# Wider products for the filter taps, later loads of the attention constants, and new instruction orders in a two-layer encoder

## The chip, the core and the metric

The kernel runs on one core of a Trainium2 chip. A core has five engines that run side by side: TensorE (PE: matrix products; its weight loads are listed as PEld), VectorE (DVE), ScalarE (ACT), GpSimd (POOL) and SyncE (SP, which here only issues transfers). Each engine takes its instructions in order and waits at the head of its queue on semaphores. Transfers from device memory run on 16 DMA engines. The metric is the device time of one launch in microseconds (us), the median of several runs.

## The reference

A hybrid encoder of two layers on an input of 256 tokens by 1024 features, all in float32:

```python
for i in range(2):
    x = x + 0.5 * swiglu(rmsnorm(x, norm_g[i, 0]), ffn_w_gate[i, 0], ffn_w_up[i, 0], ffn_w_down[i, 0])
    h = rmsnorm(x, norm_g[i, 1])
    if i == 0:   # mixer: pooling over 4 windows | order-2 Hyena (long convolutions with generated filters)
        proj = h @ mix_w_in
        x = x + concat(pool_mixer(proj[:512]), hyena_mixer(proj[512:], spectra)) @ mix_w_out
    else:        # latent attention, 16 heads, low-rank q and kv, one rotary key
        x = x + mla_mixer(h, ...)
    x = x + 0.5 * swiglu(rmsnorm(x, norm_g[i, 2]), ffn_w_gate[i, 1], ffn_w_up[i, 1], ffn_w_down[i, 1])
return rmsnorm(x, final_norm_g)
```

A feed-forward block is `(silu(h @ w_gate) * (h @ w_up)) @ w_down` with 2816 hidden features. The Hyena filters come from a small network on position features: three layers of width 64 with a sine, then `h @ w_out` (64 to 2048: two orders, two directions, 512 channels), times a decay window, then normalised by energy and transformed. The product with `w_out` is what the code calls the taps.

## The kernel before

Every float32 product is made of three products in a reduced-precision float32 format: an operand is split into a high part and a low part, and high by high, low by high and high by low are summed (`mm3`, lines 265 to 267). A split is a copy on ScalarE (`split_hi`, line 246, tiles `wh`, `ph`, `xTh`) and a subtraction on VectorE or GpSimd (`split_lo`, line 250, tiles `wl`, `pl`, `xTl`). All weights are streamed from device memory in units of 1 MB: a transfer into one of two `raw` buffers, then the split into one of four `wh`/`wl` buffer pairs, then the products. There are four PSUM banks `mm` and four `acc`.

The stages follow one another on TensorE: first feed-forward block, mixer, second block, third block, attention, fourth block. The filter work of the mixer depends on no token, so its 21 steps (`filter_steps`) are hung into the first block: `FILTERS` gives for each step the number of the hook at which it is issued; one hook follows each gate/up chunk and each half of a down chunk. Hooks 5, 8 and 11 follow the gate/up products of chunks 2, 3 and 4; hooks 6 and 7 follow the two halves of down chunk 1, hooks 9 and 10 those of down chunk 2, hooks 12 and 13 those of down chunk 3. Steps 7 and 8 are `wout` (split of the last hidden layer and of `w_out`) and `taps(0)`; then come `energy(0)`, `taps(1)`, `energy(1)`, `norm(0)`, `scaled(0)`, `norm(1)`, the tables, `dft(0, 0)`, `dft(0, 1)`, `scaled(1)`, `dft(1, 0)`, `dft(1, 1)`.

In the taps, `lo` holds the low part of the hidden layer in partitions 64 to 127 and its full value in 0 to 63, so that `lo` by `wh` over 128 partitions gives two of the three products; the third is `hi` by `wl` over partitions 0 to 63.

In the mixer, in attention and at the very start every engine's order is written out by hand in a string (`START`, `MIX`, `MLA`); a token is a letter for an operation and numbers for its unit, piece or tile, and each engine takes its own instructions in the order of the string. In `MIX`: `I` loads a unit, `h` is a high piece on ScalarE, `l` and `g` are a low piece on VectorE and on GpSimd, `P` projects, `A` is the output product, `F` adds it to x, `J` transposes x for the next block and multiplies by its gain, `j` splits that, `B` and `R` make the norm's factor. Units 12 and 13 hold the first gate weights of the second block. In `MLA`: `C` compresses to the latents, `l` and `m` turn and split the last quarter of x, `a`, `b`, `c`, `d` are norm moments, rotary key, normalisation and split of the latents, `w`, `x` and `y` are high pieces and low pieces on VectorE and on GpSimd, `I` and `i` are the low parts of queries on GpSimd and VectorE, and `Y` and `z` those of the heads' outputs. `BUFFERS` lists which buffer each tile takes, in order of allocation.

In the feed-forward blocks the instructions are placed by the scheduler of the framework, which follows its own estimate of when operands are ready; the last quarter of x, `late_now`, is transposed there with high priority. That scheduler also places what stands outside the strings, such as the four transfers of attention's constants (`ckr`, `cqt` and the two halves of `gb`, lines 1002 to 1007, issued by GpSimd) and the clearing of the value tiles (line 1020, GpSimd): in the code they stand near the end of the third block, in the trace they run as soon as the memory of the mixer's tiles is free.

Of the kernel before, what the change touches and what calls it, by code (L numbers as in the profile page):

```python
# [12 lines left out]
F32 = mybir.dt.float32  # L13
# [8 lines left out]
P = 128  # L22
D = 1024
S = 256
# [20 lines left out]
)  # L45
MIX = (
# [11 lines left out]
)  # L58
MLA = (
# [16 lines left out]
)  # L76

FILTERS = 0, 3, 3, 3, 5, 5, 5, 6, 6, 7, 7, 7, 8, 9, 9, 10, 10, 10, 12, 13, 15

BUFFERS = {  # L80
    "mm": (
        "0123012301231023013132103213021302132013201320132012301230123012031203102310231023102312032103201320",
        "1302130213201320312031023102130231023102130213023102312031201320130213201320132120312012312132013021",
        "320313103210231203100132013201321032103201320123012310231032102",
    ),
    "acc": (
        "01230123012301320103123023102310231023102310231230310321032",
    ),
    "raw": (
        "0101010101010101010101010101010101010101010101010101010101010101010101010101010101010101010101010101",  # L90
        "010101010101010101010101010101010101010101010101010101010",
    ),
    "wh": (
        "0123012301230123012301230123012301230123021302130213021302130213021302130213021302130213021302130213",
        "0213021302130213021301230123012301230123012301230123012",
    ),
    "wl": (
        "0123012301230123012301230123012301230123021302130213021302130213021302130213021302130213021302130213",
        "0213021302130213021301230123012301230123012301230123012",
    ),  # L100
    "ph": (
        "012340123401234012342432014032410324103241032413024130241304213041240134203120342103421034210",
    ),
    "pl": (
        "012340123401234012342432014032410324103241032413024130241304213401204312041304120341203412034",
    ),
    "s": (
        "0120120120120120120120201201210212120102102101220120120120120120120120120120120120120120120121021021",
        "2010210210210210210212",
    ),  # L110
    "h": (
        "0123012301230123012301230123012301230123012301230123012302103210312310231023102",
    ),
    "cu": (
        "0110010110010101",
    ),
    "cv": (
        "011001010100",
    ),
    "cw": (  # L120
        "01010101011011001010",
    ),
}
MAGIC = 12582912.0
# [50 lines left out]
def turns(t):  # L175

    return slice(t, S, 2)


class Net:  # L180
# [391 lines left out]
    def filter_steps(self, hy, fl):  # L572

        nc, a = self.nc, self.a
# [64 lines left out]
        def wout():  # L639

            hi, lo = self.pl()
            nc.scalar.activation(hi[:, :S], st["h"], AF.Copy)
            nc.vector.tensor_tensor(out=lo[64:, :S], in0=st["h"][64:], in1=hi[64:, :S].bitcast(F32), op=ALU.subtract)
            nc.scalar.activation(lo[:64, :S], st["h"][:64], AF.Copy)
            st["h3"] = (hi, lo)
            st["wo"] = self.unit([(lambda raw, r=r: raw[r], a["hyena_ffn_w_out"][0]) for r in (slice(64), slice(64, P))], U)

        def taps(o):
            def go():
                hi, lo = st["h3"]  # L650
                wh, wl = st["wo"]
                for t in range(NT):
                    for d in range(2):
                        c = slice((2 * o + d) * W, (2 * o + d + 1) * W)
                        ps = self.bank()
                        nc.tensor.matmul(out=ps, lhsT=lo[:, turns(t)], rhs=wh[:, c], start=True, stop=False)
                        nc.tensor.matmul(out=ps, lhsT=hi[:64, turns(t)], rhs=wl[:64, c], start=False, stop=True)
                        e = E[o].rearrange("p (t x) s -> p t (x s)", t=2)[:, t, d * W:(d + 1) * W]
                        nc.vector.tensor_tensor(out=e, in0=ps, in1=e, op=ALU.mult)
            return go  # L660
# [330 lines left out]
            pre += units[12], units[13]  # L991


    def mla(self, ml, cur, nxt, wg, pre, hold, dump=None):

        nc, a, x = self.nc, self.a, self.x
        r, ms = cur["r"], cur["ms"]
# [1 line left out]
        NQ, NKV = 256, 160  # L999
        small = lambda name, n=2: ml.tile([P, n], F32, name=name, bufs=4)  # L1000
        ckr = ml.tile([P, 2, 64], F32, name="ckr")
        nc.gpsimd.dma_start(out=ckr, in_=a["c_kr"])
        cqt = ml.tile([P, 2, S], F32, name="cqt")
        nc.gpsimd.dma_start(out=cqt, in_=a["c_q"])
        gb = ml.tile([P, NQ + P], F32, name="gb")
        nc.gpsimd.dma_start(out=gb[:, :NQ], in_=a["mla_q_norm_g"].to_broadcast([P, NQ]))
        nc.gpsimd.dma_start(out=gb[:, NQ:], in_=a["mla_kv_norm_g"].to_broadcast([P, P]))

# [333 lines left out]
def encoder(ctx, tc, a, out, upto=99, dbg=None):  # L1342
    nc = tc.nc
# [101 lines left out]
    with tc.tile_pool(name="ml", bufs=1) as ml:  # L1445
        finish, mid = then(1, 1)
        _, nxt = then(1, 2)
        pre = [], []
        mla = N.mla(ml, mid, nxt, a["ffn_w_gate"][1, 1], *pre, None if upto > 5 else dump)
        ffn(1, 0, cur, finish if upto > 4 else dump, mid=lambda: next(mla))  # L1450
        if upto == 4:
            return
        for _ in mla:
            pass
        if upto == 5:
            return
        cur = nxt
# [28 lines left out]
```

## Time and profile before

| | |
|---|---|
| median of 3 runs | 978.87 us (977.22 to 979.04) |
| the profiled execution | 981.94 us; 980.1 us from its first to its last instruction |
| mean granted TensorE clock | 0.992 of full speed |
| PE busy | 959.8 us, 98% of the span |
| DVE, ACT, POOL busy | 595.3, 495.3, 181.3 us |

A busy PE is a union of overlapping matmuls, so it is not yet a full PE: how densely the starts of the products follow one another says more than the busy share.

### The profile page before, as it was taken

How to read it: one execution, taken by the hardware profiler on the slowest of the kernel's cores; microseconds unless marked ns; L12 is line 12 of the kernel's file. 1: busy time of each engine (PE TensorE's matmuls, PEld its weight loads, DVE VectorE, ACT ScalarE, POOL GpSimd, SP SyncE). 2: the span in 40 equal slices, each digit the busy share in tenths (PEclk: the TensorE clock that was granted, in tenths of full speed). 3: DMA queues.
4: the chain of work that ended last, by engine and by line, in shares of the span. 5: the costliest groups of instructions: out<-in, count | busy, mean ns of one | idle time of the engine just before them, and what ended most of it. 6: DMA issues, size and time to landing. Idle time of an engine off the chain costs nothing.

```text
span 980.1 us, 12375 instructions
## 1 busy us (share of the span) xinstructions
PE 959.8 (98%) x4792; PEld 804.6 (82%) x4792; DVE 595.3 (61%) x778; ACT 495.3 (51%) x780; POOL 181.3 (18%) x231
## 2 busy tenths in 40 slices
PE   9999999999999999999999999999899999999997
PEld 6878787889997788888888888888799988888885
DVE  5577677767886644554476445554677565454454
ACT  5565554446554544443454344444578665434442
POOL 1400433316665200000000000000256520000000
PEclk9999999999999899999999999999999999999999
DMA  7757566435234654565527654565142276556531
GB/s 258 239 177 217 181 206 210 157 102 158 82 127 142 224 206 171 172 215 204 182 90 253 207 180 172 172 214 182 55 135 86 88 236 215 179 178 213 203 129 43
DMA packets 80778, 168.09 MB, mean 172 GB/s; under 512 B 3820, under 2 KB 24181, under 8 KB 80336
## 3 DMA queue, kind: packets, MB, share of 16 engines
q1 hardware_dynamic: 79232, 164.79, 49.7%
q0 software_dynamic: 1200, 1.99, 0.8%
q8 instruction: 37, 0.61, 0.2%
q10 hardware_dynamic: 288, 0.52, 0.1%
q14 instruction: 21, 0.17, 0.0%
HBM read 165.72 MB, written 1.05 MB: 170 GB/s over the span
## 4 chain that ended last, share of the span: by engine, by line
PE 81%; DVE 8%; ACT 4%; DMA 3%; issue 3%; POOL 1%; SPq 0%; POOLq 0%; DVEq 0%; ACTq 0%
PE mm L265 16%; PE mm L266 16%; PE mm L267 16%; PE acc L267 8%; PE acc L266 8%; PE acc L265 8%; PE mm L270 4%; DVE wl L250 2%; DMA raw<-ffn_w_up 2%; ACT wh L246 2%; DMA raw<-mix_w_in 1%; DVE pl L250 1%; ACT ph L246 1%; DVE s L869 0%; PE mm L1267 0%
## 5 line engine op out<-in xcount | busy, mean ns | idle before, releaser
L250 DVE TENSOR_TENSOR wl<-raw,wh 128x1024 fp32r<-128x1024 f32 (+3 forms) x321 | 358.3, 1145 | 267.5 <-ACT wh L246 267.4
L246 ACT ACTIVATE wh<-raw 128x1024 fp32r<-128x1024 f32 (+3 forms) x370 | 319.3, 903 | 285.6 <-PE mm L267 109.8
L265 PE MATMUL mm<-wh,xTh 128*128 128x512 f32 x704 | 278.1, 395 | 1.5 <-DVE s L719 1.5
L266 PE MATMUL mm<-wl,xTh 128*128 128x512 f32 x704 | 275.5, 391 | 0.2 <-DVE wl L250 0.2
L267 PE MATMUL mm<-wh,xTl 128*128 128x512 f32 x704 | 275.6, 391 | 0.0
L265 PEld LDWEIGHTS mm<-wh,xTh 128*128 128x128 f32 x704 | 133.1, 189 | 29.3 <-DVE s L719 1.9
L266 PEld LDWEIGHTS mm<-wl,xTh 128*128 128x128 f32 x704 | 133.0, 189 | 27.9 <-DVE wl L250 0.5
L267 PEld LDWEIGHTS mm<-wh,xTl 128*128 128x128 f32 x704 | 132.9, 189 | 28.0
L265 PE MATMUL acc<-wh,ph 128*128 128x512 f32 x352 | 140.0, 398 | 0.0
L267 PE MATMUL acc<-wh,pl 128*128 128x512 f32 x352 | 137.8, 391 | 0.3 <-DVE pl L250 0.3
L266 PE MATMUL acc<-wl,ph 128*128 128x512 f32 x352 | 137.9, 392 | 0.0
L273 POOL TENSOR_TENSOR r<-ms,mhalf 128x1 f32<-128x1 f32 x14 | 11.7, 842 | 583.7 <-DVE ms L295 583.7
L267 PEld LDWEIGHTS acc<-wh,pl 128*128 128x128 f32 x352 | 66.1, 188 | 14.5 <-DVE pl L250 0.8
L266 PEld LDWEIGHTS acc<-wl,ph 128*128 128x128 f32 x352 | 66.2, 188 | 12.9 <-issue 0.2
L265 PEld LDWEIGHTS acc<-wh,ph 128*128 128x128 f32 x352 | 66.1, 188 | 13.0 <-issue 0.4
L250 POOL TENSOR_TENSOR wl<-raw,wh 128x512 fp32r<-128x512 f32 (+3 forms) x49 | 64.4, 1326 | 24.8 <-ACT wh L246 24.6
L422 ACT ACTIVATE s<-mm,r 128x512 f32<-128x512 f32 (+1 forms) x48 | 31.3, 652 | 66.0 <-PE mm L267 61.7
L250 DVE TENSOR_TENSOR pl<-mm,ph 128x512 fp32r<-128x512 f32 (+1 forms) x66 | 42.9, 653 | 16.1 <-ACT ph L246 15.9
L424 DVE SCALAR_TENSOR_TENSOR h<-mm,r,s 128x512 f32<-128x512 f32 (+1 forms) x48 | 33.7, 703 | 24.5 <-PE mm L267 19.0
L246 ACT ACTIVATE ph<-mm 128x512 fp32r<-128x512 f32 (+1 forms) x66 | 36.8, 561 | 22.4 <-PE mm L270 22.3
L787 PE MATMUL acc<-xTh,wh 128*128 128x256 f32 x128 | 36.9, 288 | 0.0
L270 PE MATMUL mm<-ident,h 128*128 128x128 f32 x240 | 36.3, 272 | 0.0
(312 smaller groups left out, 1095.9 us busy)
## 6 DMA issues: line engine op xcount, KB each, us to landing
raw<-ffn_w_down SPq DMA_DIRECT2D x44, 1024.0 KB, 4.8
raw<-ffn_w_up SPq DMA_DIRECT2D x39, 1024.0 KB, 5.0
raw<-ffn_w_gate SPq DMA_DIRECT2D x38, 1024.0 KB, 5.0
raw<-mix_w_in SPq DMA_DIRECT2D x8, 1024.0 KB, 5.5
raw<-ffn_w_gate SPq DMA_DIRECT2D x8, 512.0 KB, 3.7
raw<-ffn_w_up SPq DMA_DIRECT2D x8, 512.0 KB, 4.7
raw<-mix_w_out SPq DMA_DIRECT2D x4, 1024.0 KB, 4.7
raw<-mla_w_o SPq DMA_DIRECT2D x4, 1024.0 KB, 4.8
```

The source lines that it names most:

```text
L246: return self.nc.scalar.activation(hi, src, AF.Copy)
L250: return eng.tensor_tensor(out=lo, in0=src, in1=hi.bitcast(F32), op=ALU.subtract)
L265: t.matmul(out=out, lhsT=xh, rhs=wh, start=start, stop=False)
L266: t.matmul(out=out, lhsT=xh, rhs=wl, start=False, stop=False)
L267: t.matmul(out=out, lhsT=xl, rhs=wh, start=False, stop=stop)
L270: self.nc.tensor.transpose(out=out, in_=in_, identity=self.ident)
L273: self.r_ins = self.nc.gpsimd.tensor_tensor(out=out, in0=in_, in1=self.mhalf[:, :1].to_broadcast(list(in_.shape)), op=ALU.pow)
L422: nc.scalar.activation(s[:, :w], ps_g, AF.Silu, scale=r[t])
L424: nc.vector.scalar_tensor_tensor(out=hh[:, :w], in0=ps_u, scalar=r[t], in1=s[:, :w], op0=ALU.mult, op1=ALU.mult)
L787: nc.tensor.matmul(out=ps, lhsT=wh[:, k], rhs=xh[:, k], start=st, stop=False)
```

## The change

Four edits. In `wout` the upper 64 partitions of `hi` are cleared by GpSimd, and in `taps` the second product runs over all 128 partitions. `FILTERS` moves `wout` from hook 6 to 5, `norm(0)` from 8 to 9, `dft(0, 1)` from 10 to 11, `scaled(1)` from 12 to 13; the last step, `dft(1, 1)`, goes from 15 to 16, and both numbers lie past the last hook inside the block, so that it follows the block either way. In `mla` the four constant tiles get a one-column copy of the third block's norm factor (`cur["r"][-1]`, passed as `after`) written by GpSimd ahead of their transfers, which therefore follow that factor. `MIX` and `MLA` are permuted (the number of tokens stays 245 and 377; three low pieces of `MIX` go from GpSimd to VectorE; in `MLA` five `Y` become `z`, three `I` become `i`, three `x` become `y`), and `BUFFERS` is dealt anew to match.

```diff
-FILTERS = 0, 3, 3, 3, 5, 5, 5, 6, 6, 7, 7, 7, 8, 9, 9, 10, 10, 10, 12, 13, 15
+FILTERS = 0, 3, 3, 3, 5, 5, 5, 5, 6, 7, 7, 7, 9, 9, 9, 10, 10, 11, 13, 13, 16
...
             nc.scalar.activation(lo[:64, :S], st["h"][:64], AF.Copy)
+            nc.gpsimd.memset(hi[64:, :S].bitcast(F32), 0.0)
...
-                        nc.tensor.matmul(out=ps, lhsT=hi[:64, turns(t)], rhs=wl[:64, c], start=False, stop=True)
+                        nc.tensor.matmul(out=ps, lhsT=hi[:, turns(t)], rhs=wl[:, c], start=False, stop=True)
...
-    def mla(self, ml, cur, nxt, wg, pre, hold, dump=None):
+    def mla(self, ml, cur, nxt, wg, pre, hold, after, dump=None):
...
+        cqt = ml.tile([P, 2, S], F32, name="cqt")
+        gb = ml.tile([P, NQ + P], F32, name="gb")
+
+        for m in (ckr[:, 0, :1], cqt[:, 0, :1], gb[:, :1], gb[:, NQ:NQ + 1]):
+            nc.gpsimd.tensor_copy(out=m, in_=after)
         nc.gpsimd.dma_start(out=ckr, in_=a["c_kr"])
-        cqt = ml.tile([P, 2, S], F32, name="cqt")
         nc.gpsimd.dma_start(out=cqt, in_=a["c_q"])
-        gb = ml.tile([P, NQ + P], F32, name="gb")
...
-        mla = N.mla(ml, mid, nxt, a["ffn_w_gate"][1, 1], *pre, None if upto > 5 else dump)
+        mla = N.mla(ml, mid, nxt, a["ffn_w_gate"][1, 1], *pre, cur["r"][-1], None if upto > 5 else dump)
```

The ends of `MIX` and the starts of `MLA`, where the prediction reads them:

```diff
 MIX, from the first product of the second half of the output on
-A0.0.1 h12.1 g11.1 A1.0.1 l11.3 h12.0 F0.0 g12.0 I13 J0.0 A0.1.1 l12.1 h12.3 j0.0 h13.2 h13.0 A1.1.1 h12.2 F0.1
-h13.1 B0.0 F1.0 l13.1 g12.3 g13.2 g12.2 B0.1 h13.3 g13.0 F1.1 J0.1 g13.3 B1.0 B1.1 J1.0 j0.1 j1.0 R1 R0
+A0.0.1 F0.0 A0.1.1 F0.1 h12.3 J0.0 I13 A1.0.1 g12.1 l12.3 j0.0 J0.1 A1.1.1 F1.0 h13.2 g12.2 h13.0 l13.0 h13.3
+B0.1 F1.1 j0.1 B0.0 g13.3 J1.0 h13.1 l13.1 B1.0 B1.1 R1 R0 l13.2 j1.0
 MLA, start
-L2 w1.1 C0.1 l a0 w1.0 b0 m w1.2 x1.1 C1.0 w1.3 C1.1 y1.0 c0 r1.0 a1.1 a1.0 w2.1 w2.2 b1 c1.1 c1.0 d0
+C0.1 w1.2 w1.1 l w1.3 m w1.0 x1.1 a0 y1.0 L2 C1.0 b0 C1.1 c0 x1.3 a1.1 a1.0 b1 c1.1 c1.0 d0
```

## Rows read from the trace of the kernel before

**Rows 1.** Busy time by stage: window, length, engines, granted clock, DMA share.
```profile
24.00:217.00 193.00, 190.99 (x857) 152.66 (x858) 136.83 (x164) 106.01 (x143) 46.84 (x45) 1.00 0.57 189
217.00:321.00 104.00, 98.58 (x721) 92.89 (x721) 80.65 (x130) 56.24 (x112) 65.75 (x103) 0.99 0.38 120
321.00:513.00 192.00, 192.00 (x865) 158.35 (x866) 102.63 (x110) 87.44 (x110) 3.29 (x5) 0.98 0.54 186
700.00:790.00 90.00, 85.53 (x584) 78.94 (x584) 65.19 (x140) 66.41 (x185) 52.87 (x61) 0.98 0.31 101
```

**Rows 2.** Waits of PE over the span: us in total, times, longest.
```profile
PE acc L270 <- DVE h L1072: 2.2, 1, 2.2
...
PE acc L267 <- DVE xTl L250: 1.3, 1, 1.3
...
PE acc L266 <- DVE wl L250: 0.8, 1, 0.8
```

**Rows 3.** The two products of the taps, by source line: duration ns min/median/max.
```profile
L656 PE MATMUL mm<-wh,pl x8: 397/502/503, 99.6 to 108.2; 128*128 128x512 f32 x8
...
L657 PE MATMUL mm<-wl,ph x8: 497/498/500, 100.1 to 108.6; 64*128 64x512 f32 x8
```

**Rows 4.** Timeline of PE around both groups of taps: start, duration, instruction.
```profile
99.65 0.47 PE L656 MATMUL mm<-wh,pl 128*128 128x512 f32 x1
...
103.40 0.40 PE L267 MATMUL acc<-wh,pl 128*128 128x512 f32 x1
...
105.46 0.39 PE L267 MATMUL acc<-wh,pl 128*128 128x512 f32 x1
105.69 0.40 PE L656 MATMUL mm<-wh,pl 128*128 128x512 f32 x1
...
109.36 0.40 PE L266 MATMUL mm<-wl,xTh 128*128 128x512 f32 x1
```

**Rows 5.** Timeline of PE, then of DVE, at the start of chunk 4.
```profile
147.52 0.39 PE L267 MATMUL mm<-ph,tl 128*128 128x512 f32 x1
149.40 0.50 PE L265 MATMUL mm<-wh,xTh 128*128 128x512 f32 x1 [1.50 <-DVE s L719]
...
147.52 1.23 DVE L250 TENSOR_TENSOR wl<-raw,wh 128x1024 fp32r<-128x1024 f32 x1 [2.34 <-ACT wh L246]
```

**Rows 6.** GpSimd's transfers (timeline); loads of units 12 and 13 (line 756).
```profile
304.90 0.57 POOL L1002 DMA_DIRECT2D ckr<-c_kr  x1 [1.71 <-DVE h L903]
...
306.53 0.54 POOL L1007 DMA_DIRECT2D gb<-mla_kv_norm_g  x1
...
L756 SPq DMA_DIRECT2D raw<-ffn_w_gate x2: 367/368/368, 303.8 to 307.7; - x2
...
DMA to landing us min/median/max: 5.2/7.0/8.7
```

**Rows 7.** Timeline at the end of the mixer: PE, ACT, DVE.
```profile
316.28 1.03 PE L270 MATMUL mm<-ident,x 128*128 128x128 f32 x8
320.92 1.12 PE L270 MATMUL mm<-ident,x 128*128 128x128 f32 x4 [3.60 <-DVE x L973]
...
316.51 2.19 ACT L246 ACTIVATE wh<-raw 128x512 fp32r<-128x512 f32 x4 [4.14 <-PE acc L267]
...
318.73 1.53 DVE L250 TENSOR_TENSOR wl<-raw,wh 128x512 fp32r<-128x512 f32 x1 [3.51 <-ACT wh L246]
320.19 0.68 DVE L973 TENSOR_TENSOR x<-acc,x 128x512 f32<-128x512 f32 x1
```

**Rows 8.** Two stretches of equal length at the start of the second block.
```profile
321.00:326.50 5.50, 5.50 (x15) 4.46 (x16) 4.39 (x9) 4.16 (x9) 2.74 (x4) 0.50 0.99 337
326.50:332.00 5.50, 5.50 (x25) 4.53 (x24) 4.14 (x4) 3.02 (x4) 0.00 (x0) 0.97 0.55 180
```

**Rows 9.** Timeline at the start of the third block: POOL, then ACT.
```profile
513.58 3.20 POOL L273 TENSOR_TENSOR r<-ms,mhalf 128x1 f32<-128x1 f32 x1 [8.87 <-DVE ms L295]
...
521.53 1.06 ACT L246 ACTIVATE wh<-raw 128x1024 fp32r<-128x1024 f32 x1 [1.71 <-DMA raw<-ffn_w_gate]
...
538.54 0.69 ACT L422 ACTIVATE s<-mm,r 128x512 f32<-128x512 f32 x1 [0.79 <-PE mm L267]
```

More of the change, by code (lines that the diff above doesn't have):

```diff
@@ L46 @@
 MIX = (
[11 rows of a table removed]
[11 rows of a table added]
 )
 MLA = (
[16 rows of a table removed]
[16 rows of a table added]
 )
-FILTERS = 0, 3, 3, 3, 5, 5, 5, 6, 6, 7, 7, 7, 8, 9, 9, 10, 10, 10, 12, 13, 15
+FILTERS = 0, 3, 3, 3, 5, 5, 5, 5, 6, 7, 7, 7, 9, 9, 9, 10, 10, 11, 13, 13, 16
 BUFFERS = {
     "mm": (
-        "0123012301231023013132103213021302132013201320132012301230123012031203102310231023102312032103201320",
-        "1302130213201320312031023102130231023102130213023102312031201320130213201320132120312012312132013021",
-        "320313103210231203100132013201321032103201320123012310231032102",
+        "0123012301231023013132103213021302132013201320132012301320132031203120321032103210321021231023102310",
+        "2301230123102310321032013201230132013201230123013201321032102310230123102310231232013203103213013210",
+        "132302301230132013021322103210320132013210321023102301230132012",
     ),
     "acc": (
-        "01230123012301320103123023102310231023102310231230310321032",
+        "01230123102301230130213030213021302130213021302012103120312",
     ),
@@ L90 @@
         "0101010101010101010101010101010101010101010101010101010101010101010101010101010101010101010101010101",
-        "010101010101010101010101010101010101010101010101010101010",
+        "010101010101010101010101011010101010101010101010101010101",
     ),
     "wh": (
-        "0123012301230123012301230123012301230123021302130213021302130213021302130213021302130213021302130213",
-        "0213021302130213021301230123012301230123012301230123012",
+        "0123012301230123013021302130213021302130231023102310231023102310231023102310231023102310231023102310",
+        "2310231023102310231021302103210321032103210321032103210",
     ),
     "wl": (
-        "0123012301230123012301230123012301230123021302130213021302130213021302130213021302130213021302130213",
-        "0213021302130213021301230123012301230123012301230123012",
+        "0123012301230123013021302130213021302130231023102310231023102310231023102310231023102310231023102310",
+        "2310231023102310231021032130213021302130213021302130213",
     ),
     "ph": (
-        "012340123401234012342432014032410324103241032413024130241304213041240134203120342103421034210",
+        "012340124301243012432342013240312403124031240314203142031423014201320410214341203412034120341",
     ),
     "pl": (
-        "012340123401234012342432014032410324103241032413024130241304213401204312041304120341203412034",
+        "012340124301243012432342013240312403124031240314203142031423014201132040423134201342013420134",
     ),
     "s": (
-        "0120120120120120120120201201210212120102102101220120120120120120120120120120120120120120120121021021",
-        "2010210210210210210212",
+        "0120120120120120120120120121021020202120120120120120120120120120120120120120120120120120120120120120",
+        "1021021021021021021020",
     ),
     "h": (
-        "0123012301230123012301230123012301230123012301230123012302103210312310231023102",
+        "0123012301230123012301230123012301230123012301230123012301203123012013201320132",
     ),
     "cu": (
-        "0110010110010101",
+        "0101100101101011",
     ),
     "cv": (
-        "011001010100",
+        "010110111010",
     ),
     "cw": (
-        "01010101011011001010",
+        "01010101010101010101",
     ),
```

54 rows, old and new, of tables (MIX, MLA) are left out of this document.

## The prediction

> **What bounds the kernel now.** I read the busy times by stage first. TensorE is busy in nearly all of every stage, and in the second block in all of it [rows 1]; VectorE, the next in line, has some 23 us to spare in the mixer (104.0 less 80.65) and 25 us in attention (90.0 less 65.19). So an edit pays only through TensorE's own time: by making its instructions follow one another more densely, by removing one of its waits, or by raising its clock. Busy time does not show the first, because matmuls overlap; therefore I went to the starts on PE's timeline. The yardstick is the spacing of plain products of 512 columns: from 103.40 to 105.46 us there are nine steps, 0.229 us each, and the step from 105.46 to 105.69 is as long [rows 4]. Against this yardstick I looked for places where starts lie further apart, and then asked the view of PE's waits, and the timelines of the other engines, what ended each. Five places stand out: the taps, the start of chunk 4, the end of the mixer, the first quarter of the second block (clock 0.50, the 1.2 GHz level), and the start of attention. The change touches all five.
>
> **Taps (second product over 128 partitions).** Each tap product of 64 or 128 rows lasts about 0.5 us where plain ones last 0.39 [rows 3, 4]. Starts say what that costs. First group: eight tap products begin at 99.65, one plain product follows, and the next starts at 103.40, so nine steps take 3.75 us; at the yardstick they would take 9 x 0.229 = 2.06. Excess 1.69. Second group: 105.69 to 109.36, 3.67 us less 2.06, excess 1.61. Together 3.3 us. Is the height of the operands the cause? The step from a plain product into the first tap (105.46 to 105.69), with 128 rows on both sides, is normal although that tap already has its strided weights; the slow steps are those between 64 and 128 rows. With 128 rows throughout I take the whole 3.3 us; lower bound 0. The columns streamed stay the same, so nothing is added on PE.
>
> The Trainium skill ("TensorE: Matmul & The Clock Gate", section "Part 2: What happens when you issue a matmul") says that a weight load's time follows its columns and that the number of rows doesn't matter, and its section "Why this matters for your kernels" that a single product of 32 rows takes as long as one of 128. Taken alone, that would make this edit worth nothing; the trace agrees about the single product but shows the alternation to be slow, so the row decides. It is kept as a rival below.
>
> The added clear on GpSimd has 64x256 elements. The nearest thing the trace has is GpSimd's work of half a microsecond (0.54 us for issuing a transfer [rows 6]); I take 0.3, bounds 0 and 0.6. It stands between the split of the hidden layer and the second tap product. GpSimd has 47 us of work in 193 there [rows 1], and `wout` now comes a half down chunk earlier (24 products, 24 x 0.229 = 5.5 us), which hides it. Without that cover PE would wait 0.3 us.
>
> **Filter steps moved.** At the start of chunk 4 the starts are 1.88 us apart instead of 0.23, an excess of 1.65 [rows 5]. The two transforms `dft(0, 0)` and `dft(0, 1)` stand there back to back and hold all four `mm` banks; the gate product needs one, which VectorE frees in L719, and VectorE's queue first holds a weight split that waited for ScalarE. With `dft(0, 1)` behind chunk 4, two banks are free and the wait goes: 1.65 us. Against it, `norm(0)` now comes 5.5 us later, in one hook with `scaled(0)`: the factor's chain through VectorE, GpSimd and ScalarE has less cover before the transform reads it. If PE's queue reaches the factor's transposes too soon, it waits for a GpSimd power (3.2 us in the longest such row [rows 9]). I take 1.65 saved, bounds 3.2 lost and 1.65 saved. `dft(1, 1)` still comes after the block: no cost.
>
> **Constants moved.** At the end of the mixer PE waits from its last eight transposes (start 316.28) to 320.92: 3.6 us by the bracket of the row, for the add L973 on VectorE [rows 7]. That add stood behind a split of unit 13 (318.73), which waited for ScalarE's copy, whose wait ended at 316.5. The profile names PE as releaser of that copy; but unit 13's buffer was last read by the first halves of the output product, long done. Its load was issued at 307.7 and took 8.7 us, so it landed at 316.4; unit 12's took 5.2 [rows 6]. Between them GpSimd issued the four constants, 304.90 to 307.07, and they shared the DMA engines. Without them I let unit 13 land after 5.2 us, 3.5 earlier: near 312.9. Its first splits are then done before the last output product ends at 316.4, so the add follows that product at once (0.68 us, beside four transposes, about 0.5 us as half of eight that take 1.03), and PE waits some 0.3 us: 3.3 saved. Bounds 0 and 3.6.
>
> PE then started the second block at the 1.2 GHz level: in 5.5 us 15 starts, against 25 in the next 5.5 us [rows 8], that is 10 x 0.229 = 2.3 us lost. The level fell after this idle stretch, the longest behind the start-up, so I count 2.3 us with it, bounds 0 and 2.8 (half of 5.5). Together 5.6 us.
>
> Where do the constants go? Behind the factor: the GpSimd row that makes it ends at 516.8 [rows 9], then four one-column copies and four issues of 0.54 us. Nothing stands behind these in GpSimd's queue until the end of the third block but the clears of the value tiles, first needed in attention. On the DMA engines they meet weights. The unit in flight then is split from 521.53 on, two pieces, done by about 525; its first product comes a half gate product (24 x 0.229 = 5.5 us) before 538.54, at 533. A delay of 3.5 us lies within those 8 us: no cost. If that cover failed it would cost up to 3.5 us.
>
> **New order of the mixer.** PE's wait of 0.8 us for a `wl` [rows 2] is at 306.38, where the second half of the output product reaches unit 11, whose low piece `l11.0` stood behind the last gating step `Z1` on VectorE; now it stands ahead of it. Counted with the first products' restart, 1.0 us saved. **New order of attention.** PE's 1.3 us wait for `xTl` [rows 2] is in `C1.1`: the split `m` stood behind moments `a0` and rotary key `b0` on VectorE; now it precedes both: 1.3 us saved. The 2.2 us for the normalised latents stays: it is the chain from the last product through squares, power and normalisation, and the new order has no more PE work to put into it. Low parts that go to VectorE: net three splits in the mixer and five heads' parts and no others in attention (three query parts come, three weight pieces leave); at 0.7 us each no more than 2.1 and 3.5 us, inside the 23 and 25 us to spare.
>
> All other places are re-dealt too, and the trace of before cannot show what new waits that makes. From below: nothing new, cost 0. From above: one wait as large as the mixer's end with its slow clock, 3.6 + 2.3 = 5.9. PE's remaining single waits were 0.8 to 2.2 us [rows 2]; I take 2.0 lost, about one of them.
>
> **Sum.** 3.3 + 1.65 + 5.6 + 1.0 + 1.3 - 2.0 = 10.85 us. Profiled execution: 981.94 - 10.85 = 971.1 (span 980.1 to 969.3). That execution lies 3.07 above the median, so the median goes from 978.87 to 968.0.
>
> **Rivals.** *The taps give nothing*: the steps stay slow, or the time comes back as a wait for weights in chunk 3, where VectorE has 137 us of work in 193 [rows 1]. Against it, the sharp change between 64 and 128 rows. 968.0 + 3.3 = 971.3. By the Trainium skill's rule on rows, cited above, it would end here.
> *Unit 13 stays late*: its 8.7 us come from other traffic. For it, the row names PE as releaser; against it, the constants stand between the two loads. 968.0 + 5.6 = 973.6.
> *The new orders wait more*: 5.9 instead of 2.0 us, or the norm's factor stops PE: 971.9 to 972.9.
> *No change* (within 0.2%, 2 us, which is about what a measurement of this kernel can tell): two of these together, 968.0 + 5.6 + 3.9 = 977.5.
> *Slower*: the clock. If spread-out waits at the start of attention keep PE at 1.2 GHz for longer, each 5.5 us there cost 2.3 [rows 8]. To lose the 10.85 us and 2 more it takes 13 / 2.3 x 5.5 = 31 us at that level, a third of attention; now its clock is 0.98 [rows 1], some 4 us at half. Such a stretch of 35 us would give 968.0 + 14.6 = 982.6.
>
> **Chances.** Forecast 0.57; taps 0.12; unit 13 0.08; orders 0.14; no change 0.05; slower 0.04. The first four are all faster than 976.9: 0.91. Range: the forecast's own runs from 964 (2.0 for new waits not lost, attention's 2.2 partly gone) to 971; up to 975 it takes in the three faster rivals. Left out: 0.09 of no change and slower and about as much for cases mixed beyond 975 or below 963.5.
>
> **What would show it.** Right: tap steps at 0.23 us and both lines at 0.39 us; no PE wait at L719; constants issued after 517, unit 13 landing in about 5 us, no PE wait for L973, clock near 1.00 at the second block's start; no wait for `xTl` in attention. Wrong: PE waits behind the factor's transposes, a second stretch at 1.2 GHz, or waits for weights after 517.

## The result, and the profile after

The changed kernel takes 963.72 us (median; 963.15 to 964.78) against 978.55 (977.22 to 979.04; the 978.87 of the table before is the median of three of these four runs) before: ratio 0.9852, 95% interval 0.9835 to 0.9869, 14.8 us faster. Forecast were 968.0 with 963.5 to 975.0, so the time lies in the range, near its lower end, and the gain was 4 us larger than forecast.

The profiled execution after took 963.41 us (span 961.6), that of before 981.94. Between these two there are 18.5 us; before's execution lay 3.4 above its median of 978.55 and after's 0.3 below its own, which leaves the 14.8. The readings by stage below are of the profiled executions and add up to 18.5.

Busy time by stage of the kernel after, the same view as [rows 1] with the stages' new borders (the third block's row is new):

```profile
24.00:211.50 187.50, 187.41 (x857) 152.79 (x858) 138.98 (x164) 105.62 (x142) 49.16 (x46) 1.00 0.58 195
211.50:308.00 96.50, 96.42 (x716) 92.10 (x716) 74.52 (x130) 56.60 (x113) 60.82 (x97) 1.00 0.41 134
308.00:494.00 186.00, 186.00 (x851) 153.39 (x850) 100.18 (x107) 83.37 (x104) 5.62 (x3) 1.00 0.55 187
494.00:679.00 185.00, 185.00 (x843) 152.81 (x843) 97.97 (x102) 84.14 (x104) 6.45 (x10) 1.00 0.55 186
679.00:769.00 90.00, 87.87 (x600) 81.86 (x599) 68.28 (x150) 67.73 (x188) 49.61 (x59) 0.98 0.35 114
```

TensorE now has nothing idle in the mixer (0.08 us of 96.5, where 5.4 of 104.0 were idle) and 2.1 us in attention (4.5 before). The granted clock reads 1.00 everywhere but in attention. All of PE's waits that the view of waits lists are these:

```profile
PE acc L270 <- DVE h L1076: 2.1, 1, 2.1
PE mm L347 <- DVE mhalf L330: 1.2, 1, 1.2
PE mm L270 <- DMA x<-x: 0.3, 1, 0.3
PE mm L266 <- DVE wl L250: 0.2, 1, 0.2
```

Before there were thirteen such lines, among them 3.6 us for L973, 1.5 for L719, 1.3 for an `xTl` and 0.8 for a `wl`; those are gone, and so are five of 0.3 to 0.7 us. The largest that is left is the normalised latents in attention, which the prediction left standing.

The next two answer to [rows 3] and [rows 4]: the tap products by source line, and PE's timeline of the second group of taps.

```profile
L657 PE MATMUL mm<-wh,pl x8: 392/394/394, 99.7 to 105.0; 128*128 128x512 f32 x8
...
L658 PE MATMUL mm<-wl,ph x8: 394/394/397, 100.2 to 105.3; 128*128 128x512 f32 x8
```

```profile
103.64 0.39 PE L657 MATMUL mm<-wh,pl 128*128 128x512 f32 x1
103.87 0.39 PE L658 MATMUL mm<-wl,ph 128*128 128x512 f32 x1
104.11 0.39 PE L657 MATMUL mm<-wh,pl 128*128 128x512 f32 x1
...
105.27 0.40 PE L658 MATMUL mm<-wl,ph 128*128 128x512 f32 x1
105.77 0.50 PE L265 MATMUL mm<-wh,xTh 128*128 128x512 f32 x1
```

The steps are 0.23 us, as between plain products, and durations fell from about 0.5 to 0.39 us. Only the step out of the group is longer (105.27 to 105.77, 0.27 us above the yardstick).

Then, for [rows 5], [rows 7] and [rows 6], timelines at three more places (PE at the start of chunk 4, PE at the end of the mixer, GpSimd behind the factor), and the loads of units 12 and 13 by their line.

```profile
142.98 0.39 PE L267 MATMUL mm<-ph,tl 128*128 128x512 f32 x1
143.21 0.39 PE L265 MATMUL mm<-wh,xTh 128*128 128x512 f32 x1
...
307.95 0.39 PE L267 MATMUL acc<-wh,xTl 128*128 128x512 f32 x1
308.18 0.60 PE L270 MATMUL mm<-ident,x 128*128 128x128 f32 x4
308.54 0.48 PE L265 MATMUL mm<-wh,xTh 128*128 128x512 f32 x1
308.85 0.40 PE L266 MATMUL mm<-wl,xTh 128*128 128x512 f32 x1
309.13 0.66 PE L270 MATMUL mm<-ident,x 128*128 128x128 f32 x4
...
498.56 3.20 POOL L273 TENSOR_TENSOR r<-ms,mhalf 128x1 f32<-128x1 f32 x1 [8.89 <-DVE ms L295]
...
502.31 0.60 POOL L1008 DMA_DIRECT2D ckr<-c_kr  x1
```

```profile
L757 SPq DMA_DIRECT2D raw<-ffn_w_gate x2: 367/368/368, 292.4 to 297.5; - x2
...
DMA to landing us min/median/max: 5.0/5.0/5.0
```

Chunk 4 follows at the normal step, the constants are issued from 502.31 on behind the factor, unit 13 lands in 5.0 us, and the mixer runs into the second block without a stop. Of the last twelve transposes only four stand ahead of the first gate product; the others come between gate products.

By the stages' borders (first gate product, first product of the mixer, of the second block, of attention, of the fourth block) the time of the two profiled executions went so: first block 209.9 to 204.4 (5.5 us saved), mixer 104.0 to 96.4 (7.6), second and third block 372.6 to 370.8 (1.85), attention 93.4 to 90.0 (3.4), fourth block 0.1, start-up nothing.

### The profile page after: what moved, and what is told of

It is laid out like the page before. It is cut to its first block, busy times and chain, and to the rows that moved or that the text cites. A ratio compares the mean times of both kernels' runs of the same rounds, so it can differ in the third digit from the quotient of the medians.

```text
span 961.6 us, 12376 instructions
## 1 busy us (share of the span) xinstructions
PE 950.8 (99%) x4792; PEld 802.0 (83%) x4792; DVE 592.1 (62%) x786; ACT 495.4 (52%) x780; POOL 179.2 (19%) x228
## 4 chain that ended last, share of the span: by engine, by line
PE 95%; DVE 2%; DMA 1%; issue 1%; ACT 1%; SPq 0%; POOLq 0%; POOL 0%; DVEq 0%; ACTq 0%
PE mm L266 18%; PE mm L265 18%; PE mm L267 18%; PE acc L265 10%; PE acc L267 10%; PE acc L266 10%; PE mm L270 4%; PE acc L789 2%; PE acc L790 1%; PE acc L788 1%; DMA raw<-ffn_w_up 1%; DVE wl L250 0%; PE mm L1272 0%; PE mm L1271 0%; PE mm L1273 0%
## 5 line engine op out<-in xcount | busy, mean ns | idle before, releaser
L250 DVE TENSOR_TENSOR wl<-raw,wh 128x1024 fp32r<-128x1024 f32 (+2 forms) x321 | 350.3, 1122 | 252.8 <-ACT wh L246 252.7
L273 POOL TENSOR_TENSOR r<-ms,mhalf 128x1 f32<-128x1 f32 x14 | 16.3, 1165 | 575.8 <-DVE ms L295 575.8
```

Of the source, the lines that this page charges most:

```text
L250: return eng.tensor_tensor(out=lo, in0=src, in1=hi.bitcast(F32), op=ALU.subtract)
L273: self.r_ins = self.nc.gpsimd.tensor_tensor(out=out, in0=in_, in1=self.mhalf[:, :1].to_broadcast(list(in_.shape)), op=ALU.pow)
```

## The experiments

Each kernel is the one of before or of after with one part changed; an order taken alone comes with the buffer numbers of its stretch. Line numbers of some shift by up to 45. Ratios are to the kernel before, timed on the same chip.

**The taps alone, in the kernel before** (`b_taps`).

```diff
-                        nc.tensor.matmul(out=ps, lhsT=hi[:64, turns(t)], rhs=wl[:64, c], start=False, stop=True)
+                        nc.tensor.matmul(out=ps, lhsT=hi[:, turns(t)], rhs=wl[:, c], start=False, stop=True)
+            nc.gpsimd.memset(hi[64:, :S].bitcast(F32), 0.0)
```

> The kernel before with the second tap product over 128 partitions and the clear of the upper half, nothing else. If the alternation between 64 and 128 rows is what made the steps slow, the 16 tap products follow one another at 0.23 us and PE has 3.3 us less in the first block: 978.6 - 3.3 = 975.3. Rival, the time comes back: the wait at the start of chunk 4 (L719) grows from 1.5 to 4.8 us and the time stays at 978.6. Rival, the rows do not matter: steps of 0.43 us stay, time unchanged.

978.42 us, ratio 0.9984 [0.9969, 1.0]: some 1.6 us, half of what the slow steps had cost, with an interval that just reaches no change. PE's and then VectorE's timeline at the end of the second group:

```profile
105.39 0.40 PE L658 MATMUL mm<-wl,ph 128*128 128x512 f32 x1
106.56 0.50 PE L265 MATMUL mm<-wh,xTh 128*128 128x512 f32 x1 [0.78 <-DVE xTl L660]
...
103.69 2.22 DVE L250 TENSOR_TENSOR wl<-raw,wh 128x1024 fp32r<-128x1024 f32 x1 [1.16 <-ACT wh L246]
105.83 2.47 DVE L660 TENSOR_TENSOR xTl<-mm,xTl 128x512 f32<-128x512 f32 x4
```

The steps are fast (0.23 us), but the next product needs a `mm` bank that VectorE frees in L660, and L660 stands behind a weight split of 2.22 us. The denser products run into that: a new wait of 0.8 us, and small ones at L280, at a `pl` and at L720 (1.8 where 1.5 was).

**The same short products, grouped by height** (`b_group`): the loop does four products of 128 rows and then four of 64, so the heights change twice in a group instead of at every product.

```diff
-                for t in range(NT):
-                    for d in range(2):
...
-                        nc.tensor.matmul(out=ps, lhsT=lo[:, turns(t)], rhs=wh[:, c], start=True, stop=False)
-                        nc.tensor.matmul(out=ps, lhsT=hi[:64, turns(t)], rhs=wl[:64, c], start=False, stop=True)
+                for t, d, c, ps in work:
+                    nc.tensor.matmul(out=ps, lhsT=lo[:, turns(t)], rhs=wh[:, c], start=True, stop=False)
+                for t, d, c, ps in work:
+                    nc.tensor.matmul(out=ps, lhsT=hi[:64, turns(t)], rhs=wl[:64, c], start=False, stop=True)
```

> The kernel before with the same 16 tap products, 64 rows in the second, but in each group the four products of 128 rows first and then the four of 64 rows, into four banks. If each change of height costs 0.2 us, two changes are left per group in place of eight: 12 x 0.2 = 2.4 us saved, 976.2, with steps of 0.23 inside each run of equal height. Rival, a product of 64 rows is slow by itself: there are as many as before, so no gain and steps of 0.43 between the four of 64 rows.

978.04 us, ratio 0.9972 [0.9958, 0.9986], 2.7 us faster. PE's timeline of the first group:

```profile
99.13 1.18 PE L654 MATMUL mm<-wh,pl 128*128 128x512 f32 x4
100.23 1.21 PE L656 MATMUL mm<-wl,ph 64*128 64x512 f32 x4
101.38 0.50 PE L266 MATMUL acc<-wl,ph 128*128 128x512 f32 x1
```

Four products of 64 rows take 1.21 us, four of 128 rows 1.18: the height itself costs nothing, the change of height does. A further thing showed here: in this execution PE waited 3.2 us for L973 at the mixer's end as before, yet the clock behind it stayed up, and instead fell at the start of chunk 4. Windows of that kernel, columns as in [rows 1]:

```profile
147.50:151.00 3.50, 3.50 (x10) 2.71 (x9) 3.24 (x4) 2.01 (x2) 2.80 (x2) 0.55 0.00 1
320.20:325.70 5.50, 5.50 (x26) 4.56 (x25) 4.24 (x9) 4.15 (x7) 2.39 (x4) 1.00 1.01 354
```

**The 64-row taps put back into the kernel after** (`a_taps64`): the first diff reversed.

```diff
-                        nc.tensor.matmul(out=ps, lhsT=hi[:, turns(t)], rhs=wl[:, c], start=False, stop=True)
+                        nc.tensor.matmul(out=ps, lhsT=hi[:64, turns(t)], rhs=wl[:64, c], start=False, stop=True)
-            nc.gpsimd.memset(hi[64:, :S].bitcast(F32), 0.0)
```

> The changed kernel with the second tap product over 64 rows again and no clear. With the filter steps in their new places nothing hides the slow steps: 14 or more steps of 0.43 in place of 0.23 us, 963.7 + 3.3 = 967.0. Rival, as in the old places, where the edit alone was worth 1.6 us by its ratio: 965.3.

966.0 us, ratio 0.9858 [0.9835, 0.9881]: 2.3 to 3.0 us more than the kernel after in its two measurements (963.72, and 963.02 below), and 2.8 more than `a_const` below, timed on the same chip. So with the new filter steps the taps keep most of the 3.3. Not all of the difference need be the steps: in this profiled execution, as in that of `b_add`, the clock also fell right behind the first group of taps (last section). What the slow steps are is seen at the weight loads (PEld); first this kernel, then the kernel after:

```profile
99.75 0.19 PEld L657 LDWEIGHTS mm<-wl,ph 64*128 64x128 f32 x1 [0.25 <-issue]
100.19 0.20 PEld L656 LDWEIGHTS mm<-wh,pl 128*128 128x128 f32 x1 [0.24 <-issue]
```

```profile
103.64 0.19 PEld L658 LDWEIGHTS mm<-wl,ph 128*128 128x128 f32 x1
103.88 0.19 PEld L657 LDWEIGHTS mm<-wh,pl 128*128 128x128 f32 x1
```

With equal heights the weights of a product (L658 at 103.87) are loaded one product ahead (from 103.64). Where the height alternates, the load starts with its own product (99.75 for both) and the loader first stands idle for 0.24 us, where 0.05 lies between two loads of equal height: the difference is the excess of each step.

**The filter steps alone** (`b_filters`), **and taken back out of the kernel after** (`a_filters`, the same lines reversed).

```diff
-FILTERS = 0, 3, 3, 3, 5, 5, 5, 6, 6, 7, 7, 7, 8, 9, 9, 10, 10, 10, 12, 13, 15
+FILTERS = 0, 3, 3, 3, 5, 5, 5, 5, 6, 7, 7, 7, 9, 9, 9, 10, 10, 11, 13, 13, 16
```

> The kernel before with the new hook numbers of the filter steps and the first block's new buffers; taps over 64 rows. The wait at the start of chunk 4 goes (1.65 us) and the entry into the taps becomes plain (0.3): 0.998 of the kernel before. Rival, the chain of the energy's factor, now with less cover, makes a new wait of up to 3.2 us: 1.001.

> The changed kernel with the old hook numbers of the filter steps (buffers of the first block as before). If the places of the steps are what lets PE keep the time that the taps give, the waits seen with the taps alone come back: 0.8 us for a bank behind taps(1), 1.8 us at the start of chunk 4 (L720), about 0.7 us in smaller ones: 963.7 + 3.3 = 967.0. Rival, the taps alone are enough and the places matter little: 963.7 to 964.7.

Alone: 977.74 us, ratio 0.998 [0.9966, 0.9994], 2.0 us; the wait of 1.5 us at chunk 4 is gone. Taken out: 966.77 us, ratio 0.9873 [0.9852, 0.9893], 3.0 to 3.8 us more than the kernel after. Of that kernel's waits these three lines came back:

```profile
PE mm L235 <- DVE s L690: 1.6, 1, 1.6
...
PE mm L235 <- DVE xTl L630: 0.8, 1, 0.8
...
PE acc L237 <- DVE pl L220: 0.3, 1, 0.3
```

The second is `b_taps`' wait (its L660). The new places thus do two things: they free banks at chunk 4, and they let the fast taps keep their gain.

**The constants alone** (`b_const`): of the change only the one-column copies, the argument `after` and the order of tiles and transfers in `mla`.

```diff
+        for m in (ckr[:, 0, :1], cqt[:, 0, :1], gb[:, :1], gb[:, NQ:NQ + 1]):
+            nc.gpsimd.tensor_copy(out=m, in_=after)
         nc.gpsimd.dma_start(out=ckr, in_=a["c_kr"])
```

> The kernel before with attention's constants loaded behind the third block's norm factor, orders unchanged. If the four transfers made unit 13 late, it lands in about 5 us after its issue in place of 8.7, PE's wait for the add L973 falls from 3.6 to about 0.3 us and the second block starts at full clock: 978.6 - 5.6 = 973.0. Rival, other traffic or the order of VectorE made it late: landing and wait stay, 978.6.

975.87 us, ratio 0.9952 [0.9933, 0.997], 4.7 us faster. The loads of units 12 and 13 there (line 756), then PE at the mixer's end:

```profile
L756 SPq DMA_DIRECT2D raw<-ffn_w_gate x2: 367/368/368, 303.5 to 307.3; - x2
...
DMA to landing us min/median/max: 5.0/5.1/5.1
```

```profile
315.93 1.60 PE L270 MATMUL mm<-ident,x 128*128 128x128 f32 x12
317.29 0.47 PE L265 MATMUL mm<-wh,xTh 128*128 128x512 f32 x1
```

Unit 13 lands in 5 us instead of 8.7, all twelve transposes run in one piece, and the clock stays at 1.00. From the last transposes' start to the first gate product it is 1.36 us; before it was 5.41 (316.28 to 321.69). That is 4.05 us, and the next two blocks gained 2.4 more. How the constants delay the load is seen in the view of DMA queues from 308.5 to 310.5 us: in the kernel before GpSimd's queue has 124 packets there and the queue of the weights 5; in `b_const`, where unit 13 was issued 0.35 us sooner, the queue of the weights has 263 and GpSimd's none.

**Only the add moved** (`b_add`): unit 13 stays late, but the second add goes ahead of the split that waits for it.

```diff
 MIX, near its end
-F1.0 l13.1 g12.3 g13.2 g12.2 B0.1 h13.3 g13.0 F1.1 J0.1
+F1.0 F1.1 l13.1 g12.3 g13.2 g12.2 B0.1 h13.3 g13.0 J0.1
```

> The kernel before with one token of the mixer's order moved: the last add F1.1 ahead of the split l13.1 on VectorE; constants where they were. If the place of the add behind that split is what turns a late load into PE's wait, unit 13 still lands late (8 to 9 us) but the add follows the last output product, PE's wait falls to about 0.3 us, and the clock at the start of the second block stays up if the idle stretch was what lowered it: 978.6 - 5.6 = 973.0; 3.3 saved if the clock falls all the same. Rival, PE needs unit 13 itself at that point: the wait only moves to its products, 978.6.

976.54 us, ratio 0.996 [0.9947, 0.9973], 3.9 us faster by the medians (5.7 in the mixer and the next two blocks of the profiled executions). Unit 13 landed after 7.1 us, and PE no longer waited for the add. A late load and its place in VectorE's queue made the wait together; removing either is enough.

**The mixer's order alone** (`b_mix`): `MIX` of after; the constants are issued as before.

```diff
 MIX, from the first product of the second half of the output on
-A0.0.1 h12.1 g11.1 A1.0.1 l11.3 h12.0 F0.0 g12.0 I13 J0.0 A0.1.1 l12.1 h12.3 j0.0 h13.2 h13.0 A1.1.1 h12.2 F0.1
-h13.1 B0.0 F1.0 l13.1 g12.3 g13.2 g12.2 B0.1 h13.3 g13.0 F1.1 J0.1 g13.3 B1.0 B1.1 J1.0 j0.1 j1.0 R1 R0
+A0.0.1 F0.0 A0.1.1 F0.1 h12.3 J0.0 I13 A1.0.1 g12.1 l12.3 j0.0 J0.1 A1.1.1 F1.0 h13.2 g12.2 h13.0 l13.0 h13.3
+B0.1 F1.1 j0.1 B0.0 g13.3 J1.0 h13.1 l13.1 B1.0 B1.1 R1 R0 l13.2 j1.0
```

> The kernel before with the mixer's new order and the buffers that go with it; constants, filter steps, taps and attention's order as before. If the order alone empties the mixer's waits, the output's late load stays (8 to 9 us) but PE's waits of 3.6, 0.8, 0.6 and 0.3 us and the smaller gaps go, 7.6 us by the two traces, and 2.3 more where the clock had fallen: 0.990 to 0.992 of the kernel before. Rival, it needs the constants' move: 4 us less gain, 0.995.

970.95 us, ratio 0.9908 [0.9888, 0.9928]: 9.0 us, the largest part. Its two loads (line 716):

```profile
L716 SPq DMA_DIRECT2D raw<-ffn_w_gate x2: 367/367/367, 297.5 to 302.6; - x2
...
DMA to landing us min/median/max: 5.1/6.9/8.7
```

Unit 13 is as late as ever (8.7 us), but issued 5.1 us earlier than before (302.6 against 307.7), and the split ahead of `F1.1` on VectorE is now `l13.0`, which needs two of ScalarE's copies, where `l13.1` stood behind four [rows 7]. The mixer takes 96.4 us and the next two blocks 370.8, both to 0.02 us as in the kernel after.

**The constants early again, in the kernel after** (`a_const`): the copies left out, so that the transfers are issued as soon as GpSimd comes to them.

```diff
-        for m in (ckr[:, 0, :1], cqt[:, 0, :1], gb[:, :1], gb[:, NQ:NQ + 1]):
-            nc.gpsimd.tensor_copy(out=m, in_=after)
```

> The changed kernel without the four copies, so that attention's constants load at the end of the mixer again. If the new order alone removes the wait, unit 13 lands late again (8 to 9 us) but is issued some 10 us before the last output product ends and nothing PE needs stands behind it: 963.7, within 1 us. Rival, the constants' move is worth here what it was worth in the old order (4.7 us by its ratio there): 968.4, with a PE wait of 2 to 4 us at the end of the mixer.

963.22 us, ratio 0.983 [0.981, 0.985], no slower than the kernel after. GpSimd's timeline, and the loads (line 757):

```profile
295.08 0.57 POOL L1006 DMA_DIRECT2D ckr<-c_kr  x1
```

```profile
L757 SPq DMA_DIRECT2D raw<-ffn_w_gate x2: 368/368/368, 292.1 to 297.2; - x2
...
DMA to landing us min/median/max: 5.1/6.7/8.3
```

The constants again slow unit 13 to 8.3 us, and nobody waits for it. In the new order their move is worth nothing.

**Attention's order alone** (`b_mla`): `MLA` of after.

```diff
 MLA, start
-L2 w1.1 C0.1 l a0 w1.0 b0 m w1.2 x1.1 C1.0 w1.3 C1.1 y1.0 c0 r1.0 a1.1 a1.0
+C0.1 w1.2 w1.1 l w1.3 m w1.0 x1.1 a0 y1.0 L2 C1.0 b0 C1.1 c0 x1.3 a1.1 a1.0
```

> The kernel before with attention's new order and the buffers that go with it, nothing else. By the two traces attention is 3.4 us shorter: 0.9965 of the kernel before, without waits for xTl (1.3 us), for the last low keys (0.7) and for the weights (0.3), and with the 2.2 us for the normalised latents still there. Rival, only the 1.3 us named in the prediction: 0.9987.

975.83 us, ratio 0.9957 [0.9939, 0.9975], 4.2 us. In its profile attention fell from 93.37 to 90.50 us: the waits for `xTl` (1.3), `kt1l` (0.7) and `rc` (0.3) went, the one for the latents stayed. In the same execution the wait at the mixer's end was 2.1 us and not 3.6, and the clock behind it stayed up (unit 13 landed after 7.2 us there, not 8.7); so of the 4.2 us only about 2.9 are attention's by the profile, and whether the rest belongs to the order or to chance stays open.

**Eight products into attention's last wait** (`a_fill`): the kernel after with `D8` in `MLA`, eight products of 512 columns that nobody reads, while PE would wait for the latents. They are added work; nothing else changes.

```diff
+        def fill(n):
...
+            for _ in range(n):
+                nc.tensor.matmul(out=ps, lhsT=xh[:, 0, halves(0)], rhs=xh[:, 0:2].rearrange("p k s -> p (k s)"), start=True, stop=True)
 MLA
-C1.1 c0 x1.3
+C1.1 c0 D8 x1.3
```

> The changed kernel with eight products more, whose result nothing reads, on PE behind the first transposes of the latents in attention, where PE waits 2.1 us for the normalised latents of the second half. They take 8 x 0.23 = 1.8 us of the wait. If the idle stretch is what lowers the clock behind it (0.56 of full speed for 3.5 us in the changed kernel's trace), the clock stays up and some 1.4 us are saved: 962.3. Rival, the clock falls all the same or the products hold up the transposes: 963.7 or some tenths more.

961.98 us (961.81 to 962.62), ratio 0.982 [0.9799, 0.9842], the lowest of all. PE's timeline in the kernel after at this place, and the window of the stretch behind it; then both of `a_fill`:

```profile
694.85 1.11 PE L270 MATMUL acc<-ident,h 128*128 128x128 f32 x4 [2.13 <-DVE h L1076]
```

```profile
695.00:698.50 3.50, 3.50 (x19) 3.47 (x20) 2.59 (x7) 2.51 (x7) 1.11 (x3) 0.56 0.44 145
```

```profile
692.16 2.09 PE L1304 MATMUL mm<-xTh 128*128 128x512 f32 x8
694.53 0.76 PE L255 MATMUL acc<-ident,h 128*128 128x128 f32 x4 [0.28 <-DVE h L1061]
```

```profile
694.50:698.00 3.50, 3.45 (x25) 3.08 (x26) 3.26 (x8) 2.57 (x8) 1.47 (x4) 1.00 0.39 123
```

The latents are no earlier, but behind the wait the clock is at the level 2.4 GHz (1.00) and not mostly at 1.2 (0.56): 25 starts in 3.5 us against 19. By the medians it is 1.0 to 1.7 us below the kernel after, timed elsewhere, and 1.2 below `a_const` on the same chip; the intervals overlap, and in the profiled executions attention is only 0.4 us shorter (89.5 against 90.0), so the size is not settled. That the products are what kept the clock up is not shown either: in `b_mix` and `b_add` it stayed up behind the same wait without them (last section).

**The kernel after once more** (`after_again`), beside `b_filters`, `b_mix` and `b_mla`.

> The changed kernel, timed beside the three below: 0.985 of the kernel before. It is the yardstick for the versions without one part, which were timed apart from it.

963.02 us, ratio 0.9825 [0.9801, 0.985]. The product of the parts without the constants (0.9908 x 0.9957 x 0.998 x 0.9984 = 0.9830) gives as much, within the intervals.

## Why the prediction held, and where its steps failed

The side and the five places were right; that the time lies in the range is in part luck, as the sum shows below. The steps one by one:

**Taps: right in mechanism and size, with a partner not named.** The steps went to 0.23 us as forecast, and the rival that the taps give nothing is out. But the 3.3 us come only together with the new filter places; alone 1.6 us are kept, because VectorE's L660 then frees banks too late. The Trainium skill ("TensorE: Matmul & The Clock Gate", section "Part 2: What happens when you issue a matmul") says that a weight load's time follows its columns and not its rows. The loads here agree, 0.19 us at 64 and at 128 rows; what was slow is that a load of another height is not taken ahead. The clear took 0.31 us, where 0.3 was taken, and hid.

**Filter steps: right.** 1.65 us forecast, 2.0 measured alone. The wait feared at the factor's transposes did not come. Taps and filter steps together saved 5.5 us in the first block, of 4.95 forecast.

**Constants: right cause, wrong account.** That the constants share the DMA engines with unit 13 and so stop PE is shown by `b_const`: 4.7 us by the medians, 6.45 in the profiled executions (4.05 at the mixer's end, 2.4 behind it), of 5.6 forecast. But the step counted these 5.6 us on the constants' move as if nothing else in the change reached the same wait. The mixer's new order reaches it, alone and wholly (`b_mix`), and with that order the move gives nothing (`a_const`). The two cures do not add; the sum did not count this wait twice, but only because the mixer's term left it to the constants.

**Mixer's order: mis-sized.** 1.0 us was forecast, 9.0 measured alone. Beside the constants' share it is worth some 3.7 us more in the mixer (100.1 us in `b_const`, 96.4 after): the waits of 0.8, 0.6 and 0.3 us and the restarts behind them, and about 1 us because eight transposes now fall behind the first gate product; half of that one comes back there (370.2 us for the next two blocks in `b_const`, 370.8 after).

**Attention's order: mis-sized.** 1.3 us forecast; 2.9 to 3.4 in the profiles. The two smaller waits, 0.7 and 0.3 us, were in the view of waits and not counted; with them the waits make 2.3, and where the other 0.6 to 1.1 us lie was not traced.

**New waits, 2.0 us lost: none came.** The re-dealt orders made no new wait that the view of waits lists, and took five small ones away.

**The sum, and the step from execution to median.** Between the profiled executions 10.85 us were forecast and 18.5 came. The 7.6 between them are 0.55 at taps and filters, 2.85 at the mixer's end, in its order and in the clock (9.45 instead of 6.6), 2.1 in attention, 2.0 of waits that did not come, and 0.1 in the fourth block. The other step that failed is that the new median would lie as far below its execution as before's did (3.07 us): it lay 0.3 above, which takes 3.4 off again. So a median 4.3 us below the forecast hides a sum that was off by nearly twice as much. The two errors met by luck: with 3.07 us taken off the new execution as forecast, the median would be 960.3, below the range.

**Smaller steps.** The clears of the value tiles were said to follow the copies in GpSimd's queue; after, they still run at 295 us, and GpSimd issues the constants at 502 on their own. Constants and weights met there without a wait, as forecast.

**The clock.** The 2.3 us behind the mixer's end were right for that execution (2.4 in `b_const`), but they are not a fixed price of that stall: behind nearly the same wait the clock fell in the kernel before (3.6 us) and in `b_taps` (3.5) and stayed up in `b_group` (3.2). In `b_filters` (3.5) it fell for a shorter time: the next two blocks took 371.8 us, against 372.6 before and 370.2 in `b_group`. Before's profiled execution, 3 us above its median, is one with a low mean clock, 0.992. Of the 20 executions of the kernel before that were timed beside `b_mix`, the three at 0.992 took 980.6 to 983.3 us and the three at 0.999 took 976.6 to 977.7. Behind which stalls each of these lost its clock is not known; but the step from execution to median goes with the clock, and the prediction took it as fixed. Attention had a stretch at the lower level before as well (0.64 from 711.5 to 715.0 us); it is still there after.

## What to carry to other kernels

Look for lost TensorE time in the spacing of starts, not in busy time, and keep consecutive products at one operand height, or group them by height. Here a late load hurt only through what stood behind it in an in-order queue (`b_add`, `a_const`): when two edits reach the same wait, price them as one, and take each part alone out of the new kernel as well as into the old one. A faster stretch asks for its buffers earlier, so move the work that frees them along with it.

## What was not expected of the hardware

- A change of operand height between neighbouring products costs about 0.2 us: 0.43 us from start to start against 0.23, with the weight load starting only with its own product. Four products of either height in a row show nothing of it (1.21 and 1.18 us).
- Four GpSimd transfers of constants lengthened a load of another queue from 5 us to between 7.1 (`b_add`) and 8.7 us (`b_mix`) wherever they fell just ahead of it.
- The granted clock went to the lower level behind a wait of 1.8 us (`b_group`, chunk 4) and of 2.1 us (after, attention). It stayed up behind one of 3.2 us (`b_group`) and behind the 2.2 us for the latents in `b_mix` and `b_add`. In `a_taps64` it fell right behind the slow taps with no wait at all; in `b_add` it fell there too, and in none of the profiles with taps of equal height. Windows of `a_taps64` behind its taps, then of `b_mix` behind its wait in attention:

```profile
102.50:106.20 3.70, 3.70 (x10) 2.73 (x11) 1.77 (x3) 1.97 (x4) 1.50 (x2) 0.58 0.15 58
```

```profile
701.50:705.00 3.50, 3.49 (x26) 3.11 (x27) 2.98 (x8) 1.48 (x5) 1.87 (x2) 1.00 0.16 37
```

What decides it stays open. In the one profiled execution of `a_fill`, with eight unread products in the wait, the level stayed up as well.
